# Inverse with the heads one below the other, rates as activations, the old state decayed ahead, and casts of y two K-tiles ahead

## The chip, the cores and the metric

The kernel runs on one core of a Trainium2 chip. The metric is the device time of one execution in microseconds, as a median over several runs. A profile of one execution tells what each engine did: TensorE (PE, with its weight loads PEld apart), VectorE (DVE), ScalarE (ACT), GpSimd (POOL) and SyncE (SP), which issues the DMAs.

## The reference, cut to what matters

One layer of a generator backbone, 256 latent tokens and 256 context tokens of width 2048, batch 1. A projection of the normalised input gives three groups of heads; the one that matters here is a bidirectional RWKV-7 recurrence with 16 heads of 64. Its scan runs over the tokens, for context first and then for the latents from the context's final state, forwards and backwards:

```
def step(s, inp):
    r_t, w_t, k_t, v_t, kk_t, a_t = inp
    sa = einsum('bhij,bhj->bhi', s, -kk_t)
    s = s * w_t[:, :, None, :] + sa[..., None] * (kk_t * a_t)[:, :, None, :] \
        + v_t[..., None] * k_t[:, :, None, :]
    return s, einsum('bhij,bhj->bhi', s, r_t)
...
a  = sigmoid(iclr_a0[d] + ad @ iclr_up[d])
kd = k * (1.0 + (a - 1.0) * k_a)
```

The outputs of both directions are added, group-normalised, gated, put beside a short convolution and a Fourier mix, and projected by `w_out`. A SwiGLU feed-forward part of width 5632 follows, and a last normalisation.

## The kernel before, in words

The program has four stages. Up to about 250 us it makes modulation vectors, the normalised input and the first projections. From about 250 to 1081 us runs `recurrence` (lines 851 to 900), which carries the change. From 1081 us on runs `phase_ffn`. Products with weights are made of three TensorE passes each: `wblock` (line 271) loads a block of weights by SyncE, casts it to a high part on ScalarE and subtracts for a low part on GpSimd or VectorE (`split`, line 264), and `mm3` runs high by high, high by low and low by high.

The recurrence works on pairs of heads, p = 0 to 7: head 0 of a pair lies on partitions 0 to 63, head 1 on 64 to 127 (`HV`, line 32). It first takes the eight pairs for the context (s = 0), then the eight for the latents (s = 1). A sequence of 256 tokens is cut into NC = 4 chunks of C = 64. For each of the 16 states, generators make the work:

- `rw_prep` (line 555) makes rates, decays and the small matrices of each chunk. At lines 614 to 619, for each direction and each of two operands, `f` is the rate on GpSimd (a multiply and an add with a column each), then its product on GpSimd, then `bk` on VectorE.
- `rw_inverse` (line 708), once for each direction, inverts a triangular 64x64 matrix for each chunk and head by five levels of doubling in f16, and then one correcting step in f32. `im` and `eb` hold the two heads of a chunk as the diagonal blocks of a 128x128 matrix whose other blocks were set to zero at the start (lines 859 to 862), so that one matmul of 128 rows serves both heads where they are the stationary operand. The products for the other operand (line 739) are 64*64, a head each. At the end of a level, ScalarE copies the results back in three casts (lines 743 to 745).
- `rw_scan` (line 765) goes over the four chunks in order, both directions at once: `rhs`, then `UV`, then the new state `w`. The new state is VectorE's sum of the product and the old state (line 812), times the decay of the chunk (line 813).
- `rw_out` and `group_norm` end a pair of the latents.

Each turn of the loop in `recurrence`, called a round here, takes one step of each live generator and then fills the round up to about 2.1 us of estimated TensorE time with steps of `fillers` (line 902): projections, the convolution, the Fourier mix, and `out_proj` (line 988). So TensorE's order is written out by hand by this loop. The orders of the other engines are a planner's, which follows the order of the program by priority and a simulated time; each of them runs its queue in order. `modvecs` (line 1050) puts products for the later modulation vectors (`macc`, line 1063) into VectorE's queue behind the last listed scan or inverse operation.

`out_proj` goes over the K-tiles of y in three parts, 8 to 15, 0 to 3 and 4 to 6, and then tile 7. Before each part it casts its K-tiles to `YH` (VectorE) and subtracts for `YL` (GpSimd), lines 1003 and 1004. `YH` and `YL` take over the buffers of the projections' input, `XH1` and `XL1`.

Of the kernel before, what the change touches and what calls it, by code (L numbers as in the profile page):

```python
# [17 lines left out]
P = 128  # L18
# [182 lines left out]
class Builder:  # L201
# [26 lines left out]
    def cst(self, name, i=0, n=None, rows=slice(0, P)):  # L228
        s, e = CC.at[name]
        return self.consts[rows, s + i:(e if n is None else s + i + n)]  # L230
# [324 lines left out]
    def rw_prep(self, st):  # L555
# [49 lines left out]
        for d in range(2):  # L605
            inc, exc, pi = exps[d]()
            aq = T(self.kv, [P, NC, 2 * C], F32, "aq", 4)
            st["AQ"].append(aq)
            V.tensor_tensor(aq[:, :, 0:C], exc, ch(kk), op=ALU.mult)
            if s:  # L610
                V.tensor_tensor(aq[:, :, C:], inc, ch(self.Y[:, p]), op=ALU.mult)
            bk = T(mp, [P, NC, 2, C], F32, "bk", 2)
            bks.append(bk)
            for i in range(2):
                f = T(mp, [P, L], F32, "f", 2)
                G.tensor_scalar(f, st["TA"][d], self.ab[:, 2 * i, p:p + 1], self.ab[:, 2 * i + 1, p:p + 1],
                                op0=ALU.mult, op1=ALU.add)
                G.tensor_tensor(f, f, u[i], op=ALU.mult)
                V.tensor_tensor(bk[:, :, i], ch(f), ch(pi), op=ALU.mult)
        yield 0.5  # L620
# [87 lines left out]
    def rw_inverse(self, st, d):  # L708

        nc, mp, cst = self.nc, self.mp, self.cst  # L710
        V, S, G, T = nc.vector, nc.scalar, nc.gpsimd, self.t
        while len(st["GA"]) <= d or self.inverted[d] < st["n"]:
            yield 0.0
        ga = st["GA"][d]
        msk = lambda l: self.bc4(self.m16[:, 6 * d + l])
        quads = [(c, h) for c in range(NC) for h in range(2)]
        im = self.im[d]
        x, eb = T(mp, [P, NC, C], F16, f"de{d}"), self.eb[d]
        for h in range(2):
            (G, V)[h].tensor_tensor(im[HV[h], :, h], ga[h][HV[h]], self.bc4(cst("i64", rows=HV[h])), op=ALU.add)  # L720
        for h in range(2):
            G.tensor_tensor(ga[h][HV[h]], ga[h][HV[h]], self.bc4(cst("i64", rows=HV[h])), op=ALU.add)
        yield 0.0
        pq = T(self.iv, [P, NC, C], F32, f"iv{d}")
        for c in range(NC):
            self.mm(pq[:, c], im[:, c].rearrange("p h t -> p (h t)"), self.i16, True, True)
        V.tensor_tensor(x, pq, msk(0), op=ALU.mult)
        for h in range(2):
            V.tensor_tensor(eb[HV[h], :, h], im[HV[h], :, h], self.bc4(self.m16[HV[h], 12 + d]), op=ALU.mult)  # L729
        yield 0.12  # L730
        sx = T(mp, [P, NC, C], F16, f"sx{d}")
        for l in range(1, 6):
            pd = T(self.iv, [P, 2, NC, C], F32, f"iv{d}")
            for c in range(NC):
                self.mm(pd[:, 0, c], im[:, c].rearrange("p h t -> p (h t)"), x[:, c], True, True)
            self.lastv = V.tensor_tensor(sx, pd[:, 0], msk(l), op=ALU.mult)
            yield 0.12
            for c, h in quads:
                self.mm(pd[HV[h], 1, c], sx[HV[h], c], eb[HV[h], c, h], True, True)
            for c in range(NC):  # L740
                self.mm(pd[:, 0, c], eb[:, c].rearrange("p h t -> p (h t)"), sx[:, c], True, True)
            if l < 5:
                S.copy(x, pd[:, 0])
                for h in range(2):
                    S.copy(eb[HV[h], :, h], pd[HV[h], 1])
            else:
                d32 = T(mp, [P, NC, C], F32, "d32")
                e32 = T(mp, [P, NC, C], F32, f"e32{d}", 2)
                S.copy(d32, pd[:, 0])
                S.copy(e32, pd[:, 1])  # L750
            yield 0.34
        pr = T(self.iv, [P, 2, NC, C], F32, f"iv{d}")
        for c, h in quads:
            self.mm(pr[HV[h], 0, c], ga[h][HV[h], c], d32[HV[h], c], True, True)
        r = T(mp, [P, NC, C], F32, "idm")
        V.tensor_tensor(r, self.bc4(cst("i64")), pr[:, 0], op=ALU.subtract)
        yield 0.6
        for c, h in quads:
            self.mm(pr[HV[h], 1, c], r[HV[h], c], e32[HV[h], c], True, True)
        V.tensor_tensor(e32, e32, pr[:, 1], op=ALU.add)  # L760
        st["E"][d] = e32
        self.inverted[d] += 1
        yield 0.6

    def rw_scan(self, st):

        nc, mp = self.nc, self.mp
        V, S, T = nc.vector, nc.scalar, self.t
        while self.done < st["n"] or None in st["E"]:
            yield 0.0  # L770
        yield 0.0
        p, s, UV, Z, AQ, E, BKT, PC = (st[k] for k in ("p", "s", "UV", "Z", "AQ", "E", "BKT", "PC"))
        W = self.wend[:, p] if s else None
        Ws = [W]
        for i in range(NC):
            cc = (i, NC - 1 - i)

            two = slice(i, 2 * NC - i, 2 * NC - 1 - 2 * i)
            zz = Z.rearrange("p d c t -> p (d c) t")[:, two]
            if W is None:  # L780
                rhs = zz
            else:
                pa = T(self.ps, [P, 2, C], F32, "st")
                for d in range(2):
                    for h in range(2):
                        self.mm(pa[HV[h], d], AQ[d][HV[h], cc[d], 0:C], W[HV[h], d], True, True)
                rhs = T(mp, [P, 2, C], F32, "rhs", 2)
                self.lastv = V.tensor_tensor(rhs, zz, pa, op=ALU.subtract)
                yield 0.29
            pu = T(self.ps, [P, 2, C], F32, "st")  # L790
            for d in range(2):
                for h in range(2):
                    self.mm(pu[HV[h], d], E[d][HV[h], cc[d]], rhs[HV[h], d], True, True)
            for h in range(2):
                u = UV[HV[h], h].rearrange("p d c t -> p (d c) t")[:, two]
                if h == 0:
                    self.lastv = V.tensor_copy(u, pu[HV[h]])
                else:
                    S.copy(u, pu[HV[h]])
            yield 0.29  # L800
            if s and i == NC - 1:
                break
            pw = T(self.ps, [P, 2, C], F32, "st")
            for d in range(2):
                for h in range(2):
                    self.mm(pw[HV[h], d], BKT[d][:, cc[d], C * h:C * h + C], UV[:, h, d, cc[d]], True, True)
            Wn = self.wend[:, p] if not s and i == NC - 1 else T(mp, [P, 2, C], F32, "w", 4)
            pc = PC[:, two].unsqueeze(2).to_broadcast([P, 2, C])
            if W is None:
                V.tensor_tensor(Wn, pw, pc, op=ALU.mult)  # L810
            else:
                V.tensor_tensor(Wn, pw, W, op=ALU.add)
                self.lastv = V.tensor_tensor(Wn, Wn, pc, op=ALU.mult)
            W = Wn
            Ws.append(W)
            yield 0.29
        if s:
            yield from self.rw_out(st, Ws)
        self.done += 1
        if s and p == 3:  # L820
            yield from self.group_norm(0, 4)
        if s and p == 6:
            yield from self.group_norm(4, 7)
        if s and p == 7:
            self.closing = True
            for _ in self.mv:
                pass
            yield from self.group_norm(7, 8)
# [22 lines left out]
    def recurrence(self):  # L851
# [3 lines left out]
        self.credit = 0.0  # L855
        self.normed = self.taken = self.valued = self.queried = self.done = 0
        self.inverted = [0, 0]

        self.im = [self.t(self.mp, [P, NC, 2, C], F16, f"im{d}") for d in range(2)]
        self.eb = [self.t(self.mp, [P, NC, 2, C], F16, f"eb{d}") for d in range(2)]  # L860
        for t in self.im + self.eb:
            self.nc.gpsimd.memset(t, 0.0)
        self.closing = self.gated = False
        for p in range(2):
            for _ in self.value(p):
# [122 lines left out]
    def out_proj(self):  # L988
# [11 lines left out]
        for k0, k1 in ((8, 16), (0, 4), (4, 7)):  # L1000
            while k0 < NP and self.normed < k1:
                yield None
            for k in range(k0, k1):
                self.split(YH[:, k], YL[:, k], self.Y[:, k], V, G)
            for n in range(KT):
                while k0 == 4 and (n >= HOLD and not self.closing or n >= KT - HOLD2 and self.normed < NP):
# [2 lines left out]
                for g in range(k0, k1, G4):  # L1009
                    m = min(G4, k1 - g)  # L1010
                    h, lo = self.wblock(self.a["wout"][n, :, g:g + m], m, G4, self.wst)
                    for j in range(m):
                        k = g + j
                        self.mm3(pj, h[:, j], lo[:, j], YH[:, k], YL[:, k], k == k0, k == k1 - 1)
                        yield MM3
                add(n, pj)
# [197 lines left out]
```

## Time and profile before

| | us |
|---|---|
| median of 3 runs | 1855.45 |
| lowest and highest run | 1853.03, 1862.34 |
| the profiled execution | 1853.2 |
| its span, first to last instruction | 1851.4 |
| TensorE busy | 1715.0 (93%) |
| TensorE weight loads busy | 1570.0 (85%) |
| VectorE busy | 1113.0 (60%) |
| ScalarE busy | 829.9 (45%) |
| GpSimd busy | 801.3 (43%) |
| mean granted clock of TensorE | 0.974 |

The profiled execution is one run of its own; its time is the span and what lies around it on the device. Matmuls are pipelined, so that the start of one group to the start of the next says what a group takes, and not its own length. An engine's idle time is put down to what ended it. Means over the span hide that the stages differ, so the stretch of the recurrence is read by itself.

### The profile page before, as it was taken

How to read it: one execution, taken by the hardware profiler on the slowest of the kernel's cores; microseconds unless marked ns; L12 is line 12 of the kernel's file. 1: busy time of each engine (PE TensorE's matmuls, PEld its weight loads, DVE VectorE, ACT ScalarE, POOL GpSimd, SP SyncE). 2: the span in 40 equal slices, each digit the busy share in tenths (PEclk: the TensorE clock that was granted, in tenths of full speed). 3: DMA queues.
4: the chain of work that ended last, by engine and by line, in shares of the span. 5: the costliest groups of instructions: out<-in, count | busy, mean ns of one | idle time of the engine just before them, and what ended most of it. 6: DMA issues, size and time to landing. Idle time of an engine off the chain costs nothing.

```text
span 1851.4 us, 44772 instructions
## 1 busy us (share of the span) xinstructions
PE 1715.0 (93%) x18552; PEld 1570.0 (85%) x18552; DVE 1113.0 (60%) x1883; ACT 829.9 (45%) x1657; POOL 801.3 (43%) x718
## 2 busy tenths in 40 slices
PE   7888999999899889898998888999999999999997
PEld 4767898888788777677786678999999999999996
DVE  4445257787888787768787488665555544333333
ACT  2113355566665554445554154444444444444442
POOL 1224455467667665656663353233222323333332
PEclk9999999999999999999999789999999999999998
DMA  9884224354545444344443137777777666565564
GB/s 335 305 273 152 75 78 129 121 161 149 160 153 159 141 135 133 107 156 137 128 134 100 46 114 233 238 240 241 231 231 231 200 194 191 186 188 189 188 188 137
DMA packets 139227, 318.74 MB, mean 172 GB/s; under 512 B 14224, under 2 KB 40464, under 8 KB 139024
## 3 DMA queue, kind: packets, MB, share of 16 engines
q1 hardware_dynamic: 137936, 314.84, 53.7%
q8 instruction: 145, 2.38, 0.5%
q10 hardware_dynamic: 1088, 1.05, 0.2%
q14 instruction: 58, 0.48, 0.1%
HBM read 313.74 MB, written 2.10 MB: 171 GB/s over the span
## 4 chain that ended last, share of the span: by engine, by line
PE 45%; DVE 8%; DMA 2%; ACT 2%; POOL 1%; issue 1%; DVEq 0%; ACTq 0%
PE gu L233 21%; PE dn L233 13%; PE pj L233 4%; DMA w<-wgu 2%; PE acc L233 2%; PE iv L233 2%; PE st L233 2%; POOL wlo L269 1%; PE pp L233 1%; DVE macc L1063 1%; DVE XL L1151 1%; ACT whi L266 1%; DVE HL L1122 0%; DVE eb L729 0%; DVE xn L1149 0%
## 5 line engine op out<-in xcount | busy, mean ns | idle before, releaser
L269 POOL TENSOR_TENSOR wlo<-w,whi 128x512 fp32r<-128x512 f32 (+2 forms) x309 | 518.6, 1681 | 712.8 <-ACT whi L266 679.7
L266 ACT CAST whi<-w 128x1024 fp32r<-128x1024 f32 (+2 forms) x472 | 401.2, 850 | 539.7 <-DMA w<-wgu 133.1
L233 PE MATMUL gu<-XH,whi 128*128 128x256 f32 (+1 forms) x1408 | 393.7, 280 | 4.2 <-ACT whi L266 3.7
L233 PE MATMUL gu<-XH,wlo 128*128 128x256 f32 (+1 forms) x1408 | 392.1, 280 | 3.6 <-POOL wlo L269 2.8
L269 DVE TENSOR_TENSOR wlo<-w,whi 128x1024 fp32r<-128x1024 f32 (+1 forms) x175 | 206.4, 1180 | 312.7 <-ACT whi L266 312.7
L233 PE MATMUL gu<-XL,whi 128*128 128x256 f32 x1344 | 372.5, 277 | 0.1
L233 PE MATMUL pj<-XH,whi 128*128 128x256 f32 x1016 | 286.5, 310 | 5.6 <-DVE XL L997 3.2
L233 PEld LDWEIGHTS gu<-XH,whi 128*128 128x128 f32 x1408 | 267.0, 190 | 5.9 <-ACT whi L266 5.2
L233 PEld LDWEIGHTS gu<-XH,wlo 128*128 128x128 f32 x1408 | 266.2, 190 | 4.6 <-POOL wlo L269 3.6
L233 PE MATMUL pj<-XL,whi 128*128 128x256 f32 x1016 | 258.5, 283 | 0.6 <-DVE XL L269 0.6
L233 PE MATMUL pj<-XH,wlo 128*128 128x256 f32 x1016 | 258.1, 282 | 0.0
L233 PEld LDWEIGHTS gu<-XL,whi 128*128 128x128 f32 x1344 | 253.8, 189 | 0.3 <-DVE XL L1151 0.3
L233 PEld LDWEIGHTS pj<-XH,whi 128*128 128x128 f32 x1016 | 182.5, 192 | 16.7 <-ACT whi L266 3.1
L233 PE MATMUL dn<-HL,whi 128*128 128x256 f32 x704 | 196.0, 278 | 0.0
L233 PE MATMUL dn<-HH,wlo 128*128 128x256 f32 x704 | 194.4, 276 | 0.0
L233 PE MATMUL dn<-HH,whi 128*128 128x256 f32 x704 | 194.3, 276 | 0.0
L233 PEld LDWEIGHTS pj<-XL,whi 128*128 128x128 f32 x1016 | 182.8, 192 | 2.4 <-issue 0.9
L233 PEld LDWEIGHTS pj<-XH,wlo 128*128 128x128 f32 x1016 | 181.8, 191 | 2.6 <-POOL whi L268 1.7
L1063 DVE SCALAR_TENSOR_TENSOR macc<-wm,sc,macc 128x512 f32<-128x512 f32 x180 | 169.9, 944 | 0.9
L233 PEld LDWEIGHTS dn<-HL,whi 128*128 128x128 f32 x704 | 132.1, 188 | 1.4
L233 PEld LDWEIGHTS dn<-HH,wlo 128*128 128x128 f32 x704 | 132.2, 188 | 0.0
L233 PEld LDWEIGHTS dn<-HH,whi 128*128 128x128 f32 x704 | 132.2, 188 | 0.0
(306 smaller groups left out, 2846.4 us busy)
## 6 DMA issues: line engine op xcount, KB each, us to landing
w<-wgu SPq DMA_DIRECT2D x176, 512.0 KB, 4.8
wm<-wmb SPq DMA_DIRECT2D x192, 256.0 KB, 3.1
w<-wdn SPq DMA_DIRECT2D x80, 512.0 KB, 4.4
w<-wib SPq DMA_DIRECT2D x148, 256.0 KB, 3.3
wm<-wma SPq DMA_DIRECT2D x64, 512.0 KB, 7.2
XH<-wmb SPq DMA_DIRECT2D x64, 256.0 KB, 5.0
w<-wout SPq DMA_DIRECT2D x48, 256.0 KB, 3.2
wa<-wia SPq DMA_DIRECT2D x16, 416.0 KB, 7.9
```

Of the source, the lines that this page charges most:

```text
L233: self.last = self.nc.tensor.matmul(out, lhsT=lhsT, rhs=rhs, start=start, stop=stop)
L266: he.copy(hi, src)
L269: le.tensor_tensor(lo, src, hi.bitcast(F32), op=ALU.subtract)
L1063: V.scalar_tensor_tensor(acc, w, self.sc[:, k, 1:2], acc, op0=ALU.mult, op1=ALU.add)
L1151: V.scalar_tensor_tensor(XL[:, k], xn, bias, XH[:, k].bitcast(F32), op0=ALU.add, op1=ALU.subtract)
```

## The change

The inverse holds the heads one below the other: `im` and `xe` (which joins `x` and `eb`) have the two heads on the two halves of the partitions and no zero blocks, and all f16 matmuls are 64*64, one for each chunk and head. The three casts of a level become one, the two masks on VectorE one, and the memsets go. The rates `f` are ScalarE activations with a scale and a bias column. In the scan, ScalarE multiplies the old state by its decay for each direction right after the state is made (`decayed`), and the new state is, for each direction, one VectorE operation: product times decay plus the decayed old state. In `out_proj` two K-tiles are cast ahead of the loop, and each further one two K-tiles before its use in the first block of columns.

```diff
--- before.py
+++ after.py
@@ -613,8 +613,8 @@
             bks.append(bk)
             for i in range(2):
                 f = T(mp, [P, L], F32, "f", 2)
-                G.tensor_scalar(f, st["TA"][d], self.ab[:, 2 * i, p:p + 1], self.ab[:, 2 * i + 1, p:p + 1],
-                                op0=ALU.mult, op1=ALU.add)
+                S.activation(f, st["TA"][d], AF.Identity, bias=self.ab[:, 2 * i + 1, p:p + 1],
+                             scale=self.ab[:, 2 * i, p:p + 1])
                 G.tensor_tensor(f, f, u[i], op=ALU.mult)
                 V.tensor_tensor(bk[:, :, i], ch(f), ch(pi), op=ALU.mult)
         yield 0.5
@@ -714,35 +714,34 @@
         ga = st["GA"][d]
         msk = lambda l: self.bc4(self.m16[:, 6 * d + l])
         quads = [(c, h) for c in range(NC) for h in range(2)]
-        im = self.im[d]
-        x, eb = T(mp, [P, NC, C], F16, f"de{d}"), self.eb[d]
+
+        im = T(mp, [P, NC, C], F16, f"im{d}")
         for h in range(2):
-            (G, V)[h].tensor_tensor(im[HV[h], :, h], ga[h][HV[h]], self.bc4(cst("i64", rows=HV[h])), op=ALU.add)
+            (G, V)[h].tensor_tensor(im[HV[h]], ga[h][HV[h]], self.bc4(cst("i64", rows=HV[h])), op=ALU.add)
         for h in range(2):
             G.tensor_tensor(ga[h][HV[h]], ga[h][HV[h]], self.bc4(cst("i64", rows=HV[h])), op=ALU.add)
         yield 0.0
         pq = T(self.iv, [P, NC, C], F32, f"iv{d}")
-        for c in range(NC):
-            self.mm(pq[:, c], im[:, c].rearrange("p h t -> p (h t)"), self.i16, True, True)
-        V.tensor_tensor(x, pq, msk(0), op=ALU.mult)
-        for h in range(2):
-            V.tensor_tensor(eb[HV[h], :, h], im[HV[h], :, h], self.bc4(self.m16[HV[h], 12 + d]), op=ALU.mult)
+        for c, h in quads:
+            self.mm(pq[HV[h], c], im[HV[h], c], self.i16[HV[h]], True, True)
+
+        xe = T(mp, [P, 2, NC, C], F16, f"de{d}")
+        V.tensor_tensor(xe[:, 0], pq, msk(0), op=ALU.mult)
+        V.tensor_tensor(xe[:, 1], im, self.bc4(self.m16[:, 12 + d]), op=ALU.mult)
         yield 0.12
         sx = T(mp, [P, NC, C], F16, f"sx{d}")
         for l in range(1, 6):
             pd = T(self.iv, [P, 2, NC, C], F32, f"iv{d}")
-            for c in range(NC):
-                self.mm(pd[:, 0, c], im[:, c].rearrange("p h t -> p (h t)"), x[:, c], True, True)
+            for c, h in quads:
+                self.mm(pd[HV[h], 0, c], im[HV[h], c], xe[HV[h], 0, c], True, True)
             self.lastv = V.tensor_tensor(sx, pd[:, 0], msk(l), op=ALU.mult)
             yield 0.12
             for c, h in quads:
-                self.mm(pd[HV[h], 1, c], sx[HV[h], c], eb[HV[h], c, h], True, True)
-            for c in range(NC):
-                self.mm(pd[:, 0, c], eb[:, c].rearrange("p h t -> p (h t)"), sx[:, c], True, True)
+                self.mm(pd[HV[h], 1, c], sx[HV[h], c], xe[HV[h], 1, c], True, True)
+            for c, h in quads:
+                self.mm(pd[HV[h], 0, c], xe[HV[h], 1, c], sx[HV[h], c], True, True)
             if l < 5:
-                S.copy(x, pd[:, 0])
-                for h in range(2):
-                    S.copy(eb[HV[h], :, h], pd[HV[h], 1])
+                S.copy(xe, pd)
             else:
                 d32 = T(mp, [P, NC, C], F32, "d32")
                 e32 = T(mp, [P, NC, C], F32, f"e32{d}", 2)
@@ -772,6 +771,16 @@
         p, s, UV, Z, AQ, E, BKT, PC = (st[k] for k in ("p", "s", "UV", "Z", "AQ", "E", "BKT", "PC"))
         W = self.wend[:, p] if s else None
         Ws = [W]
+        pcs = lambda i, d: PC[:, (2 * NC - 1 - i if d else i):(2 * NC - i if d else i + 1)]
+
+        def decayed(W, i):
+
+            w = T(mp, [P, 2, C], F32, "wp", 2)
+            for d in range(2):
+                S.mul(w[:, d], W[:, d], pcs(i, d))
+            return w
+
+        Wp = decayed(W, 0) if s else None
         for i in range(NC):
             cc = (i, NC - 1 - i)
 
@@ -805,14 +814,15 @@
                 for h in range(2):
                     self.mm(pw[HV[h], d], BKT[d][:, cc[d], C * h:C * h + C], UV[:, h, d, cc[d]], True, True)
             Wn = self.wend[:, p] if not s and i == NC - 1 else T(mp, [P, 2, C], F32, "w", 4)
-            pc = PC[:, two].unsqueeze(2).to_broadcast([P, 2, C])
             if W is None:
-                V.tensor_tensor(Wn, pw, pc, op=ALU.mult)
+                V.tensor_tensor(Wn, pw, PC[:, two].unsqueeze(2).to_broadcast([P, 2, C]), op=ALU.mult)
             else:
-                V.tensor_tensor(Wn, pw, W, op=ALU.add)
-                self.lastv = V.tensor_tensor(Wn, Wn, pc, op=ALU.mult)
+                for d in range(2):
+                    self.lastv = V.scalar_tensor_tensor(Wn[:, d], pw[:, d], pcs(i, d), Wp[:, d], op0=ALU.mult, op1=ALU.add)
             W = Wn
             Ws.append(W)
+            if i < NC - 1:
+                Wp = decayed(W, i + 1)
             yield 0.29
         if s:
             yield from self.rw_out(st, Ws)
@@ -855,11 +865,6 @@
         self.credit = 0.0
         self.normed = self.taken = self.valued = self.queried = self.done = 0
         self.inverted = [0, 0]
-
-        self.im = [self.t(self.mp, [P, NC, 2, C], F16, f"im{d}") for d in range(2)]
-        self.eb = [self.t(self.mp, [P, NC, 2, C], F16, f"eb{d}") for d in range(2)]
-        for t in self.im + self.eb:
-            self.nc.gpsimd.memset(t, 0.0)
         self.closing = self.gated = False
         for p in range(2):
             for _ in self.value(p):
@@ -1000,7 +1005,7 @@
         for k0, k1 in ((8, 16), (0, 4), (4, 7)):
             while k0 < NP and self.normed < k1:
                 yield None
-            for k in range(k0, k1):
+            for k in range(k0, k0 + 2):
                 self.split(YH[:, k], YL[:, k], self.Y[:, k], V, G)
             for n in range(KT):
                 while k0 == 4 and (n >= HOLD and not self.closing or n >= KT - HOLD2 and self.normed < NP):
@@ -1011,6 +1016,8 @@
                     h, lo = self.wblock(self.a["wout"][n, :, g:g + m], m, G4, self.wst)
                     for j in range(m):
                         k = g + j
+                        if n == 0 and k + 2 < k1:
+                            self.split(YH[:, k + 2], YL[:, k + 2], self.Y[:, k + 2], V, G)
                         self.mm3(pj, h[:, j], lo[:, j], YH[:, k], YL[:, k], k == k0, k == k1 - 1)
                         yield MM3
                 add(n, pj)
```

## Rows read from the trace of the kernel before

**Rows 1.** The page: busy us, share of the span, instructions.

```profile
PE 1715.0 (93%) x18552; PEld 1570.0 (85%) x18552; DVE 1113.0 (60%) x1883; ACT 829.9 (45%) x1657; POOL 801.3 (43%) x718
```

**Rows 2.** Stretches: length; PE, PEld, DVE, ACT, POOL busy; clock; DMA.

```profile
250.00:1000.00 750.00, 686.74 (x9345) 599.67 (x9344) 580.25 (x1150) 409.13 (x1043) 462.56 (x518) 0.97 0.45 138
```

**Rows 3.** TensorE's waits, 250 to 1000 us: total us, times, longest us.

```profile
PE iv L233 <- DVE idm L756: 20.4, 15, 3.5
PE st L233 <- DVE w L813: 11.2, 9, 5.3
...
PE st L233 <- ACT UV L799: 3.9, 6, 1.1
PE iv L233 <- ACT e L750: 3.9, 3, 1.8
```

**Rows 4.** TensorE in order of time, 303 to 309 us: start, length, group.

```profile
302.97 1.15 PE L233 MATMUL pp<-UV,ga 64*64 64x64 f32 x32
...
304.95 0.45 PE L233 MATMUL st<-w,aq 64*64 64x64 f32 x8
305.23 0.29 PE L233 MATMUL iv<-eb,sx 64*64 64x64 f16 x8
305.46 0.29 PE L233 MATMUL iv<-sx,eb 128*128 128x64 f16 x4
305.58 0.28 PE L233 MATMUL iv<-de,im 128*128 128x64 f16 x4
...
307.28 0.45 PE L233 MATMUL st<-rhs,e 64*64 64x64 f32 x8
307.66 0.29 PE L233 MATMUL iv<-de,im 128*128 128x64 f16 x4
307.88 0.31 PE L233 MATMUL iv<-eb,sx 64*64 64x64 f16 x8
```

**Rows 5.** TensorE in order of time, an f32 group of 256 columns.

```profile
792.71 1.89 PE L233 MATMUL pj<-XL 128*128 128x256 f32 x8
```

**Rows 6.** ScalarE's groups, whole span: shapes, count | busy us, mean ns | idle.

```profile
L745 ACT CAST eb<-iv 64x256 f16<-64x256 f32 x256 | 93.8, 366 | 3.1
L743 ACT CAST de<-iv 128x256 f16<-128x256 f32 x128 | 47.5, 371 | 70.4 <-PE iv L233 44.5 <-issue 15.1 <-ACT whi L266 7.6
L649 ACT COPY bkt<-pp 128x512 f32<-128x512 f32 x32 | 17.8, 588 | 31.5 <-PE pp L646 31.2
L468 ACT ACTIVATE xn<-xn,m 128x256 f32<-128x256 f32 x32 | 17.5, 592 | 123.6 <-DVE m L463 123.6
L799 ACT COPY UV<-st 64x128 f32<-64x128 f32 x64 | 16.7, 260 | 58.2 <-DVE UV L797 57.4
L684 ACT ACTIVATE ta<-pp,ha 128x256 f32<-128x256 f32 x32 | 14.9, 467 | 0.0
```

**Rows 7.** VectorE's and GpSimd's groups, whole span, same columns.

```profile
L729 DVE TENSOR_TENSOR eb<-im,m 64x256 f16<-64x256 f16 x64 | 34.5, 540 | 3.4 <-POOL im L720 1.6
L997 DVE SCALAR_TENSOR_TENSOR XL<-pj,mod,XL 128x256 f32<-128x256 f32 x56 | 26.7, 479 | 20.8 <-PE pj L233 20.3
L813 DVE TENSOR_TENSOR w<-w,pc 128x128 f32<-128x128 f32 x40 | 26.1, 652 | 0.6
L812 DVE TENSOR_TENSOR w<-st,w 128x128 f32<-128x128 f32 x32 | 9.2, 288 | 19.1 <-PE st L233 19.1
L1077 DVE TENSOR_TENSOR mod<-pj,vecs 128x4 f32<-128x4 f32 x12 | 1.9, 159 | 11.9 <-PE pj L233 11.9
...
L616 POOL TENSOR_SCALAR f<-ta,ab 128x256 f32<-128x256 f32 x64 | 50.6, 797 | 41.3 <-ACT ta L684 26.9 <-DVE bk L619 11.5 <-ACT tw L686 2.4
```

**Rows 8.** VectorE in order of time, 777 to 785 us.

```profile
777.76 2.43 DVE L268 CAST XH<-XH 128x256 fp32r<-128x256 f32 x5 [0.27 <-PE pj L233]
...
783.16 0.81 DVE L813 TENSOR_TENSOR w<-w,pc 128x128 f32<-128x128 f32 x1
```

**Rows 9.** A stretch after that wait, same columns as rows 2.

```profile
784.10:791.50 7.40, 7.39 (x54) 5.21 (x54) 3.43 (x7) 3.53 (x10) 3.07 (x6) 0.50 0.21 64
```

## The prediction

> **What bounds the kernel now.** I read the page's busy times first, then the stretches, then who waits for whom, then the orders of TensorE and VectorE themselves. The page shows TensorE busy 93% of the span [rows 1]. The change touches the recurrence alone, and nearly all of that lies between 250 and 1000 us. There TensorE is busy 686.74 of 750 us, VectorE 580.25, GpSimd 462.56, ScalarE 409.13 [rows 2]. So TensorE sets the pace, and 750 - 686.74 = 63 us of it is waiting. The waits are almost all for VectorE and ScalarE that come late: 20.4 us for `idm` of the inverse, 11.2 us for the new state `w` (one alone 5.3 us), 3.9 us each for `UV` and `e` [rows 3]. TensorE's own order is written out by hand, so a late operand stops all that stands behind it. Two things can therefore shorten the stage: fewer TensorE slots, and operands that come in time.
>
> **The change part by part.** All sums are against the profiled execution, 1853.2 us (span 1851.4, 1.8 us around it); the median of the runs is 2.25 us higher, 1855.45, and I add that at the end.
>
> *Heads one below the other, on TensorE.* Now each inverse has eleven groups of four 128-row matmuls with 64 columns (one for the transposition, two for each of five levels), 32 x 11 = 352. Each becomes eight 64*64 matmuls. Does twice the number cost twice the time? In the order of TensorE [rows 4] four 128-row ones take 305.46 to 305.58 = 0.12 us, and the eight 64*64 ones that exist already take 305.23 to 305.46 = 0.23 us. But this 0.23 holds a second thing. A group `st` of eight is followed by a 64*64 group after 0.28 us (304.95 to 305.23) and by a 128-row group after 0.38 us (307.28 to 307.66). A 128-row group is followed by a 64*64 one after 0.22 us (307.66 to 307.88), not 0.12. So a turn between the two shapes costs about 0.10 us in either direction, and eight 64*64 ones alone take 0.23 - 0.10 = 0.13 us: the two heads run beside each other. That they can is shown by f32: eight 128-row matmuls of 256 columns take 1.89 us, which is 0.236 each or 0.059 us for 64 columns [rows 5], while 32 64*64 ones of 64 columns take 1.15 us with their pipeline, 0.036 each [rows 4]. So the groups cost 352 x 0.01 = 3.5 us more, and what counts is the turns. Inside a level 128, 64, 128 become 64, 64, 64. Going through TensorE's order from 250 to 1085 us, I count 681 turns between neighbours without idle time between them; with every inverse group as 64*64 the same order has 483. A round such as that from 307.28 loses two of three turns; one such as that from 304.95 keeps one, since the turn moves behind the group. 198 x 0.10 = 20 us less. Together **-17 us**; bounds: -24 us (every turn at 0.12) and, if TensorE idles in those turns anyway, 0.
>
> A rule of the Trainium skill speaks against this: "TensorEngine Tiling (Array Packing)", section Instruction Overhead, gives each matmul a fixed cost of about 60 cycles and warns against tiling where the dimension is small already; at 64 columns eight small ones would then cost twice four. No row here separates issue from streaming; what it would make of the time is the last rival.
>
> *Heads one below the other, on ScalarE and VectorE.* At four levels of 32 inverses, three casts (371 + 2 x 366 = 1103 ns) become one of 128x512 [rows 6]. The nearest row is the copy of that size, 588 ns; upper end two 128x256 casts, 742. So 128 x 0.515 = 66 us of ScalarE go. The next level's first matmul needs the cast: 371 ns for `x` before, but `pd`'s buffer was free only after all three, so the new 588 ns is no later. On VectorE two masks of 540 ns become one of the same columns: 32 x 0.54 = 17 us go [rows 7]. The four memsets lie in the first stage beside GpSimd's idle time: nothing.
>
> *Rates as activations.* 64 GpSimd operations of 797 ns, 51 us, go; ScalarE gets 64 of 467 ns (nearest: `ta`, an activation with a bias column; ends 366, the cast of as many columns, and 592 [rows 6]), 30 us. This is the front of the chain rate, product, `bk`, behind which VectorE, in order, holds `e` and `idm`. I take **-5 us** of the 20.4 + 3.9 us of waits [rows 3]; ends 0 and -20.
>
> *Old state times its decay ahead.* 48 steps lose a sum of 288 and a product of 652 ns and get two `scalar_tensor_tensor` of 128x64 out of PSUM [rows 7]. No row has one; below is 159 ns (128x4), above 288 (128x128), and I take 240: on the line from 159 ns at 4 columns to the 479 ns of such an operation at 256, 64 columns give 235. The step's end comes 0.94 - 0.48 = 0.46 us earlier, and VectorE loses 22 us. Of the 11.2 us for `w` 5.9 remain beside the long one, in eight waits of about 0.7 us, and two like them lie in the tail after 1000 us: 10 x 0.4 = **-4 us**; ends 0 and -8. ScalarE gets 112 multiplications (8 heads' pairs x 3 steps x 2 and x 4 x 2, the last unused), 112 x 0.23 = 26 us, the duration between nothing and the 260 ns of the 64x128 copy. None is needed for three rounds, but each waits for VectorE's new `w`, and behind it on ScalarE stand the casts of weights and the evictions of `UV`, `iv` and `pp`. ScalarE's sum is -66 + 30 + 26 = -10 us, so its load does not grow, but its order gets new waits. I take **+2 us**; ends 0 and +44 (all 176 new operations at 0.25 us on the path).
>
> *Casts of y.* At 777.7 us the last reader of the buffer ends and VectorE casts five K-tiles in 2.43 us, two more follow, and only then it makes the state `w` (783.16) [rows 8], for which TensorE waits 5.3 us [rows 3]. The clock then stands at 0.50, the lower of its two levels, over 784.1 to 791.5 us, in which TensorE is busy 7.39 us [rows 9]; at the upper level the same work would take half, so up to 3.7 us more are lost. With two casts ahead and the others behind the first weight block, the product is ahead of most of them. **-6 us** of the at most -9; end 0 if the scheduler pulls the ready casts forward again. The two later bursts (four and three casts) come one by one already, as their tiles are finished.
>
> Sum: -17 - 5 - 4 + 2 - 6 = -30 us: 1853.2 - 30 = 1823 us profiled, and 1825 us as a median of runs. VectorE loses about 40 of 580 us, about as TensorE does, so VectorE stays as tight as it is: that is why I take only a quarter of the `idm` waits.
>
> **The rivals.** (1) *VectorE takes the pace.* It is busy 77% already, and its order is a planner's. If freed slots turn into waits of the same kind, half of the turns and the casts remain: -8 - 4 = -12, 1843 us. For: 63 us of waits in a stage that TensorE should bind. Against: each edit takes work off VectorE. (2) *Nothing comes through*: turns lie in front of waits, the casts bunch up again; 1850 to 1860 us. Against: the 681 turns counted are those without idle time. (3) *ScalarE in its order.* The multiplications wait for `w`, and evictions wait behind them. 112 + 64 operations at 0.25 us, all of it on the path, give +44 - 17 - 6 = +21: 1876 us. It decides against the change from about 27 us on, that is when six in ten of them delay something that TensorE takes next. For: the waits for `UV` and `e` show that ScalarE's evictions can be late. Against: ScalarE is busy 409 of 750 us. (4) *The small matmuls do not pair.* Eight at 0.03 us each, as the four 128-row ones are spaced, would also make 0.24 us, near the 0.23 seen; then each group costs 0.11 us more, 352 x 0.11 = +39 us, less the 13 us of the other parts: 1881 us. Against: the f32 rows, which cannot be had one by one.
>
> **How the numbers follow.** Forecast (1805 to 1840 us) 0.55; a gain smaller or larger that still counts, mostly rival 1, 0.18; rival 2 0.14; rivals 3 and 4 0.13 together. About 0.5%, 9 us, is what a measurement of this kernel can tell from no change. Below 1846 us lie the forecast and most of rival 1: faster 0.72. Same 0.15. Slower 0.13. The lower end is all terms at their ends but the waits for `idm` half: -24 - 10 - 8 - 9 = -51, 1804; I go to 1800. The upper end reaches over rival 1 into rival 2: 1851. The likeliest case's own range is 1805 to 1840.
>
> **What would show it.** In the trace after: a round of inverse groups between two `st` groups without the 0.38 us step, eight 64*64 groups following each other in 0.13 us, not 0.24 (else rival 4); one cast of about 0.6 us for each level; no wait of 5 us near 780 us and no half clock behind it; `w` made in two operations of at most 0.29 us; waits for `idm` below 20 us. If waits for ScalarE (`UV`, `e`, casts of weights) exceed 15 us, rival 3 is at work. If TensorE's waits in the recurrence stay above 60 us while its groups shorten, it is rival 1.

## The result and the profile after

The changed kernel takes 1835.52 us as a median (1833.69 to 1839.64, 4 runs), the kernel before beside it 1858.89 us. The ratio is 0.9879, with an interval of 0.9843 to 0.9914. A later run of the same program gave 1833.83 us and 0.9854 (0.9819 to 0.9889). So 22 to 27 us are gone, where 30 were forecast; 1835.5 us lies in the range of 1805 to 1840, ten above the 1825 that were named.

The page of the changed kernel, busy times as in [rows 1]:

```profile
PE 1702.9 (93%) x19960; PEld 1566.8 (86%) x19960; DVE 1068.0 (58%) x1851; ACT 827.7 (45%) x1577; POOL 744.5 (41%) x650
```

The recurrence's stretch after, columns of [rows 2]:

```profile
250.00:1000.00 750.00, 690.82 (x10997) 608.83 (x10996) 547.88 (x1135) 411.98 (x973) 410.11 (x457) 0.97 0.45 139
```

VectorE loses 32 us of this stretch, GpSimd 52, ScalarE gains 3; TensorE stays the one that paces, with 59 us of waiting instead of 63. But the 750 us hold more of the work than before, so the stage is better taken whole. From the first inverse matmul to the first of the feed-forward part it was 258.43 to 1081.53 us, and is 258.89 to 1064.08: 823.1 us became 805.2. These two stretches, before and then after, columns of [rows 2]:

```profile
258.43:1081.53 823.10, 747.49 (x9996) 644.98 (x9995) 617.56 (x1240) 434.97 (x1105) 476.42 (x530) 0.96 0.43 130
```

```profile
258.89:1064.08 805.19, 736.63 (x11404) 642.50 (x11403) 578.35 (x1207) 430.91 (x1020) 422.79 (x469) 0.96 0.44 133
```

TensorE is busy 10.9 us less and waits 7.0 us less (75.6 to 68.6). The feed-forward part is 2 us shorter, without any edit in it. So 18 of the 19.5 us between the two spans come from the recurrence.

TensorE in order of time after, start, length, group:

```profile
439.49 0.45 PE L233 MATMUL st<-rhs,e 64*64 64x64 f32 x8
439.77 0.29 PE L233 MATMUL iv<-de,sx 64*64 64x64 f16 x8
439.89 0.29 PE L233 MATMUL iv<-sx,de 64*64 64x64 f16 x8
440.02 0.29 PE L233 MATMUL iv<-de,im 64*64 64x64 f16 x8
440.24 0.39 PE L233 MATMUL pj<-XH,whi 128*128 128x256 f32 x1
```

Eight 64*64 matmuls take 0.12 and 0.13 us when another 64*64 group follows, and 0.22 us when `pj` with 128 rows follows. That is the turn of 0.10 us, now behind the groups. Between neighbours without idle time I count 500 turns from 250 us to the end of the recurrence, where 681 were and 483 were forecast. The count hangs on what is called a turn: by every change of rows or columns it is 888 before and 732 after, by a change of columns alone 619 and 468, so 151 to 181 turns are gone.

Waits of TensorE after, 250 to 1000 us, columns of [rows 3]:

```profile
PE iv L233 <- DVE idm L755: 25.3, 14, 4.2
PE iv L233 <- DVE de L729: 6.0, 6, 2.2
...
PE iv L233 <- ACT de L744: 4.3, 9, 1.6
...
PE st L233 <- DVE w L821: 3.0, 3, 2.1
PE st L233 <- ACT UV L808: 2.1, 4, 0.8
PE iv L233 <- ACT e L749: 1.0, 2, 0.7
```

The wait for the state fell from 11.2 to 3.0 us, those for ScalarE's `UV` and `e` by 4.7 us together; the one for a level's cast is 4.3 us (2.2 before, for `eb`), and the one for `idm` rose from 20.4 to 25.3.

The new operations on ScalarE and VectorE, columns of [rows 6] and [rows 7]:

```profile
L744 ACT CAST de<-iv 128x512 f16<-128x512 f32 x128 | 74.2, 579 | 29.9 <-PE iv L233 19.7 <-issue 3.7 <-ACT whi L266 2.1
L616 ACT ACTIVATE f<-ta,ab 128x256 f32<-128x256 f32 x64 | 35.9, 598 | 5.1 <-DVE bk L619 5.0
L780 ACT ACTIVATE wp<-w,pc 128x64 f32<-128x64 f32 x96 | 30.3, 344 | 40.2 <-DVE w L821 31.9 <-DVE w L818 8.2
```

```profile
L730 DVE TENSOR_TENSOR de<-im,m 128x256 f16<-128x256 f16 x32 | 20.3, 634 | 2.9 <-POOL im L720 1.1
L821 DVE SCALAR_TENSOR_TENSOR w<-st,pc,wp 128x64 f32<-128x64 f32 x80 | 18.9, 277 | 19.9 <-PE st L233 19.9
```

### The profile page after: what moved, and what is told of

Same layout as the page of the kernel before. It is cut to its first block, busy times and chain, and to the rows that moved or that the text cites. A ratio compares the mean times of both kernels' runs of the same rounds, so it can differ in the third digit from the quotient of the medians.

```text
span 1831.9 us, 47450 instructions
## 1 busy us (share of the span) xinstructions
PE 1702.9 (93%) x19960; PEld 1566.8 (86%) x19960; DVE 1068.0 (58%) x1851; ACT 827.7 (45%) x1577; POOL 744.5 (41%) x650
## 4 chain that ended last, share of the span: by engine, by line
PE 72%; DVE 14%; ACT 5%; issue 4%; POOL 1%; DMA 0%; DVEq 0%; ACTq 0%; POOLq 0%
PE gu L233 25%; PE pj L233 17%; PE dn L233 13%; PE iv L233 4%; PE pp L233 4%; PE st L233 3%; PE acc L233 3%; DVE macc L1070 2%; PE pacc L233 1%; DVE m L463 1%; DVE im L720 1%; DVE XL L1158 1%; DVE bk L619 1%; ACT xn L468 1%; DVE HL L1129 1%
## 5 line engine op out<-in xcount | busy, mean ns | idle before, releaser
L269 POOL TENSOR_TENSOR wlo<-w,whi 128x512 fp32r<-128x512 f32 (+2 forms) x309 | 515.4, 1671 | 750.2 <-ACT whi L266 722.9
L233 PE MATMUL pj<-XH,whi 128*128 128x256 f32 x1016 | 290.9, 315 | 3.3 <-DVE XL L1002 1.6
L1070 DVE SCALAR_TENSOR_TENSOR macc<-wm,sc,macc 128x512 f32<-128x512 f32 x180 | 163.9, 910 | 1.9 <-DMA wm<-wmb 1.1
```

What stands on the lines that cost most here:

```text
L233: self.last = self.nc.tensor.matmul(out, lhsT=lhsT, rhs=rhs, start=start, stop=stop)
L269: le.tensor_tensor(lo, src, hi.bitcast(F32), op=ALU.subtract)
L1070: V.scalar_tensor_tensor(acc, w, self.sc[:, k, 1:2], acc, op0=ALU.mult, op1=ALU.add)
```

## The experiments

Each time is a median of 5 to 12 executions, beside the kernel before on the same chip. Runs under one heading shared a chip, but for the last one; over chips, ratios are compared, since the median of before lay between 1855.24 and 1860.68 us.

### The four parts one at a time

The inverse alone:

```diff
-            for c in range(NC):
-                self.mm(pd[:, 0, c], im[:, c].rearrange("p h t -> p (h t)"), x[:, c], True, True)
+            for c, h in quads:
+                self.mm(pd[HV[h], 0, c], im[HV[h], c], xe[HV[h], 0, c], True, True)
...
-                S.copy(x, pd[:, 0])
-                for h in range(2):
-                    S.copy(eb[HV[h], :, h], pd[HV[h], 1])
+                S.copy(xe, pd)
```

> The kernel before with the new inverse alone (64*64 f16 matmuls, one cast a level, one mask, no zero blocks). Theory (TensorE's turns): about 180 of 681 turns between the shapes go at 0.10 us, 352 groups cost 0.01 us more: 12 to 18 us faster than before, so most of the 22 us of the whole change. Rival (VectorE's relief): the gain comes from VectorE's shorter queue, of which this part has 17 us of 45: less than 9 us faster, and TensorE's waits grow by what the turns give.

Measured: 1849.75 us, 0.9937 (0.9914 to 0.9961), against 1859.69.

The decay alone (buffer single):

```diff
+            w = T(mp, [P, 2, C], F32, "wp", 1)
+            for d in range(2):
+                S.mul(w[:, d], W[:, d], pcs(i, d))
...
-                V.tensor_tensor(Wn, pw, W, op=ALU.add)
-                self.lastv = V.tensor_tensor(Wn, Wn, pc, op=ALU.mult)
+                for d in range(2):
+                    self.lastv = V.scalar_tensor_tensor(Wn[:, d], pw[:, d], pcs(i, d), Wp[:, d], op0=ALU.mult, op1=ALU.add)
```

> The kernel before with the old state decayed ahead alone (its buffer single instead of double, for space). Theory: the waits for the state w fall from 11 us to about 3, of which some come back as other waits: 3 to 8 us faster. Rival (VectorE's relief): this part takes 21 us off VectorE, the most of all parts: 9 us or more faster.

Measured: 1861.73 us, 1.0021 (0.9986 to 1.0056): no gain, against theory and rival alike.

The rates alone:

```diff
-                G.tensor_scalar(f, st["TA"][d], self.ab[:, 2 * i, p:p + 1], self.ab[:, 2 * i + 1, p:p + 1],
-                                op0=ALU.mult, op1=ALU.add)
+                S.activation(f, st["TA"][d], AF.Identity, bias=self.ab[:, 2 * i + 1, p:p + 1],
+                             scale=self.ab[:, 2 * i, p:p + 1])
```

> The kernel before with the rates as ScalarE activations alone. Theory: GpSimd was not what TensorE waited for, and the product behind the rate still stands on GpSimd: within 4 us of before, either sign, waits for idm not below 18 us. Rival (VectorE's relief): VectorE's operations with two SBUF operands shorten without 51 us of GpSimd beside them: 5 us or more faster.

Measured: 1867.05 us, 1.0046 (1.0019 to 1.0073): slower, by about 8 us, more than the theory allowed; and the waits for `idm` fell below its 18 us.

The casts alone:

```diff
-            for k in range(k0, k1):
+            for k in range(k0, k0 + 2):
...
+                        if n == 0 and k + 2 < k1:
+                            self.split(YH[:, k + 2], YL[:, k + 2], self.Y[:, k + 2], V, G)
```

> The kernel before with the casts of y two K-tiles ahead alone. Theory: the planner still takes the ready casts as soon as their buffer is free, seven of eight within 8 us as in the changed kernel: within 3 us of before, and a wait of TensorE of several us near 780 us stays. Rival: the two-ahead order itself took 5.3 to 2.1 us of that wait and shortened the half clock: 4 to 9 us faster.

Measured: 1864.31 us, 1.0009 (0.9976 to 1.0041), with the wait of 5.3 us still there: no gain, as the theory says, though the median is 4.6 us above that of before.

What follows: only the inverse gains alone, 12 us by the ratio (7 to 16) and 10 by the medians, the least of what the turns promised. That is above the rival's bound of 9, but the interval reaches below it. The other three together give 0.0076 of loss, so the four alone add up to 1.0013, but together they gave 0.9879 and 0.9854. Neither theory had this: the parts depend on each other. The recurrence itself, from its first inverse matmul to the first feed-forward one, says the same; it is taken from one profiled execution each, and two of the same program differ by 3.7 us. The feed-forward part, which no edit touches, took 787 and 786 us in the traces of the decay and the casts alone and 770 in that of the kernel before, so whole times scatter for reasons outside the change. The clock is the mean granted clock over all executions that were timed, with that of the kernel before beside it.

| | recurrence, us | TensorE busy | waiting | clock | clock of before |
|---|---|---|---|---|---|
| before | 823.1 | 747.5 | 75.6 | | |
| inverse alone | 819.5 | 746.3 | 73.2 | 0.9662 | 0.9719 |
| decay alone | 825.4 | 757.4 | 68.0 | 0.9691 | 0.9719 |
| rates alone | 828.3 | 750.2 | 78.1 | 0.9701 | 0.9719 |
| casts alone | 819.4 | 743.3 | 76.2 | 0.9733 | 0.9719 |
| changed kernel | 805.2 | 736.6 | 68.6 | | |
| the same again | 808.9 | 743.8 | 65.0 | 0.9722 | 0.9712 |

The granted clock is a rival that no run puts to the test. The inverse alone ran at a lower clock than the kernel before, and the decay alone took 7.6 us of waiting away and had 9.9 us more of busy TensorE. An estimate from this table: if TensorE loses what the mean clock loses, the four alone lose 0.0089 of the time to it in sum, while the whole change gains 0.0010. That is 18 us of the 25 to 30 by which the sum of the parts misses the whole. No run parts the clock from the waits, so which of them comes first stays open.

Waits of TensorE with the rates alone, 250 to 1000 us:

```profile
PE iv L233 <- DVE idm L756: 17.2, 13, 2.2
...
PE st L233 <- ACT UV L799: 6.8, 10, 1.8
PE iv L233 <- ACT eb L745: 6.3, 11, 1.7
```

The last two were 3.9 us [rows 3] and 2.2 us before. ScalarE is busy 436 us of the stretch there instead of 409. That gave the next theory: the rates and the multiplications need room on ScalarE, and the merged cast makes it. For the multiplications the trace does not bear it out: with the decay alone ScalarE is busy 436 us too, and the waits for `UV` and `eb` there are 2.5 and 2.3 us.

### The parts taken out of the changed kernel

First the changed kernel again:

> The changed kernel as it is, on the same chip as the next three. Every theory: as measured, about 0.988 of before.

Measured: 1833.83 us, 0.9854 (0.9819 to 0.9889), against 1860.68.

Without the rates (the diff above reversed):

> The changed kernel with the rates back on GpSimd. Theory (ScalarE's room): alone the rates cost 8 us because ScalarE, 30 us fuller, came late with UV and the casts; in the changed kernel the merged cast pays for that, so taking them back changes little: 0.986 to 0.991 of before. Rival (the parts add): 8 us faster than the changed kernel, 0.984 or less of before. Second rival (the parts need each other through VectorE): slower than the changed kernel, 0.992 or more.

Measured: 1844.29 us, 0.9920 (0.9896 to 0.9943). The second rival's bound is met: in the changed kernel the rates are worth about 10 us by the medians, 8 to 12 by the ratios. Its waits:

```profile
PE iv L233 <- DVE idm L755: 25.9, 18, 3.1
PE iv L233 <- DVE sx L737: 6.4, 10, 1.7
```

The wait for `sx` was 3.9 us with the rates on ScalarE; the waits for ScalarE are 5.6 us in sum here and 8.1 there. So the room on ScalarE says why the rates cost nothing in the changed kernel, and not what they gain. The clock was 0.9690, against 0.9722 for the changed kernel on the same chip, an estimated 6 us of the 10.

Without the decay ahead:

> The changed kernel with the old two VectorE operations for the new state. Theory (ScalarE's room): alone it gave nothing because 35 us of multiplications went to ScalarE; with room there the shorter path shows: 4 to 8 us slower than the changed kernel, 0.990 to 0.993 of before. Rival (the parts add): alone it gave nothing, so nothing is lost: 0.986 to 0.989.

Measured: 1837.68 us, 0.9879 (0.9847 to 0.9912), 4 us by the medians, with intervals that overlap: at the theory's lower edge in us and within the rival's range in the ratio, so open. The long wait for the state is back:

```profile
PE st L233 <- DVE w L812: 8.5, 8, 5.5
```

With three casts a level:

```diff
-                S.copy(xe, pd)
+                S.copy(xe[:, 0], pd[:, 0])
+                for h in range(2):
+                    S.copy(xe[HV[h], 1], pd[HV[h], 1])
```

> The changed kernel with each level's cast in three pieces again, 64*64 matmuls and all else kept: ScalarE gets 66 us back. Theory (ScalarE's room): the evictions come late again and at least 8 us of the gain go: 0.992 or more of before, waits for ScalarE's casts and UV over 12 us. Rival (TensorE's turns are all): the turns are kept and ScalarE is off the path: 0.987 to 0.990.

Measured: 1845.44 us, 0.9920 (0.9890 to 0.9950), as the theory says. Its waits for ScalarE:

```profile
PE iv L233 <- ACT de L746: 13.7, 19, 2.2
...
PE iv L233 <- ACT e L751: 2.0, 4, 0.8
PE pj L233 <- ACT u L574: 2.0, 1, 2.0
PE st L233 <- ACT UV L810: 1.7, 2, 1.2
```

The turns are the same there and the matmuls too, and the clock, 0.9714, is nearly that of the changed kernel. So about 11 us of the inverse's worth in the changed kernel is the merged cast, by way of ScalarE. Two ways lead there, and no run parts them: 59 us less of load on ScalarE in the stretch (471 to 412), or the end of a level's copies, for which the next level's first matmul waits, 0.5 us sooner (three casts, 1103 ns together, against one of 579).

### The theory of room, the casts held, and idm

Three casts and the rates on GpSimd at once:

> The changed kernel with each level's cast in three pieces and with the rates on GpSimd. Taken back singly, each cost 0.0066 of the time. Theory (ScalarE's room: the rates pay only while ScalarE has room for them): without room there is nothing to lose with the rates, so both together cost about as much as one: 0.990 to 0.994 of before, waits for ScalarE 10 to 14 us as in the kernel before. Rival (two separate gains): both are lost, 0.997 or more.

Measured: 1845.78 us, 0.9948 (0.9926 to 0.9970), against 1855.24. Taken one by one the two cost 0.0066 each; both cost 0.0094 in the ratio against 0.9854. It lies between one loss (0.9920) and two (0.9986), just beyond the theory's 0.994 and short of the rival's 0.997; the interval holds both. The waits for a level's cast are 8.5 us, less than with three casts and the rates on ScalarE (13.7). So the rates seem to pay less where ScalarE is full; whether they pay nothing there stays open. No run has the turns alone either. This one comes nearest, with the turns, the decay, the single mask and the casts of y: 0.9948 is 10 us, 6 to 14 by the interval, where the turns counted below make 12 to 15; but its clock was 0.9696 where before had 0.9747.

The casts of y held behind the scan:

```diff
+                            with self.tc.issue_after(self.lastv.ins):
+                                self.split(YH[:, k + 2], YL[:, k + 2], self.Y[:, k + 2], V, G)
```

> The changed kernel with each cast of y that is made in the loop held behind the last scan operation recorded before it, so that the planner cannot take five at once. Theory (the casts bunched up because they were ready): the waits near 770 to 790 us for w, sx and the cast of a level (2.1, 0.7, 0.7 and 1.6 us) and the half clock behind them go: 3 to 8 us faster than the changed kernel, 0.981 to 0.984 of before. Rival (they only move: VectorE is as full either way): within 2 us of the changed kernel.

Measured: 1837.70 us, 0.9915 (0.9885 to 0.9945). Now two casts stand at 771 us and the others at 784 to 789 us, and the ratio is no lower than that of the changed kernel (0.9854 and 0.9879), if anything a little higher. The theory is out. That they only move, as the rival says, fits the recurrence in the traces (804.6 us against 805.2 and 808.9); the ratio is above the rival's bound of 2 us.

The products for the modulation vectors behind `idm`:

```diff
-        V.tensor_tensor(r, self.bc4(cst("i64")), pr[:, 0], op=ALU.subtract)
+        self.lastv = V.tensor_tensor(r, self.bc4(cst("i64")), pr[:, 0], op=ALU.subtract)
...
-        V.tensor_tensor(e32, e32, pr[:, 1], op=ALU.add)
+        self.lastv = V.tensor_tensor(e32, e32, pr[:, 1], op=ALU.add)
```

> The changed kernel with the products for the modulation vectors queued also behind idm and the last sum of an inverse, the two operations for which TensorE waits longest; macc stands among the three operations ahead of idm 13 times instead of 31. Theory (TensorE waits for idm because VectorE's queue holds macc before it): the waits for idm fall from 25 us to 15 or less, 5 to 12 us faster than the changed kernel. Rival (idm waits behind bk, which waits for GpSimd's product): waits for idm stay above 20 us and the time within 3 us.

Measured: 1825.03 us (1823.13 to 1828.06), 0.9837 (0.9807 to 0.9867), 12.7 us below the run with the casts held on the same chip. It is below the changed kernel too, by 3 to 8 us in the ratios, with intervals that overlap. Its recurrence took 794.4 us in the trace, against 804.6 with the casts held and 805.2 and 808.9 in the changed kernel. The clock was 0.9738, against 0.9705 with the casts held. Its waits:

```profile
PE iv L233 <- DVE idm L755: 9.1, 8, 2.7
PE pp L233 <- DVE mq L639: 7.4, 7, 3.0
```

More of the same:

```diff
-                V.tensor_tensor(gt, pg[:, :, 0:C], ...
+                self.lastv = V.tensor_tensor(gt, pg[:, :, 0:C], ...
...
-                    V.tensor_tensor(mq[:, h], pg[:, :, C:], ...
+                    self.lastv = V.tensor_tensor(mq[:, h], pg[:, :, C:], ...
...
-        V.tensor_tensor(xe[:, 1], im, ...
+        self.lastv = V.tensor_tensor(xe[:, 1], im, ...
```

> The changed kernel with macc queued behind idm and the last sum of an inverse, and further behind the masks ga and mq of the preparation and the second mask of an inverse. In the three operations ahead macc now stands 7 times instead of 19 before mq and 26 instead of 58 before ga, but 45 instead of 29 times before the first masks of an inverse. Theory (each wait goes that macc is taken away from): the 11 us of waits for mq halve, 3 to 6 us faster than with idm alone, about 0.981 of before. Rival (macc has to stand before something): the waits for the masks of the inverse grow by as much, within 3 us of the run with idm alone, 0.982 to 0.986.

Measured: 1829.67 us, 0.9850 (0.9820 to 0.9880), against 1856.11. Nothing is gained over `idm` alone. The wait for `mq` shown above fell from 7.4 to 3.8 us, and others came, though not those that the rival expected:

```profile
PE st L233 <- ACT UV L808: 8.9, 10, 2.5
PE st L233 <- DVE rhs L797: 7.2, 5, 2.6
PE st L233 <- DVE w L818: 6.4, 3, 2.5
```

## Why the prediction came out, point by point

**The turns (-17 us).** The mechanism held in the trace: 0.12 to 0.13 us for eight, 0.22 before a turn, 151 to 181 turns gone where 198 were forecast. At 0.10 us each, less 352 x 0.01, that is 12 to 15 us; TensorE's busy time in the recurrence fell by 10.9 us, in the second profiled execution by 3.7. Two small slips in the prediction change nothing: its own terms, 20 less 3.5, make 16 and not 17, and 0.236 us for an f32 matmul is the length of a group, with its pipeline, by eight; from start to start it is 0.22. The rule of a fixed cost for each matmul, in the Trainium skill's "TensorEngine Tiling (Array Packing)", section Instruction Overhead, taken by itself would have had the eight cost twice the four; the trace does not agree for pairs that lie on different halves of the array, so rival 4 is out. The inverse alone, merged cast included, measured 12 us; what the turns alone bring in time no run shows.

**ScalarE's sum and the merged cast.** The cast measured 579 ns (588 taken). The rates measured 598 ns, above the upper end of 592, and the multiplications 344 ns, above their upper end of 260. So ScalarE was not relieved by 10 us, its busy time stayed (409 to 412 us in the stretch). The prediction put the cast's relief off the path. That step failed: with three casts 11 us come back, and the waits for ScalarE are 22 us instead of 8, over the mark of 15 that rival 3 had; the changed kernel stays under it. Whether that is ScalarE's load or the later end of a level's copies stays open.

**Rates (-5 us for `idm`).** Half right alone, wrong in the whole. With the rates alone the wait for `idm` fell by 3.2 us, and more came back as waits for ScalarE. In the changed kernel it is 25.3 us with them and 25.9 without, and yet they are worth 10 us there and cost 8 us alone. `bk`, which was to come sooner, takes longer: 701 ns in the mean, 635 before. Moving work to another engine had no fixed price here. Part of it is how full that engine was, part the clock, and the rest is open.

**The decay (-4 us).** The waits for `w` fell by 8.2 us, of which 3.2 us are in the one long wait near 780 us; the operation takes 277 ns instead of 240. Taken out, it costs 4 us by the medians, alone it gave nothing. The shorter path to the state is shown, and the forecast size is not contradicted; that it gains time is not shown.

**The casts (-6 us).** Wrong; the end at nothing, which the prediction named, is what happened. VectorE in order of time after:

```profile
769.77 2.40 DVE L268 CAST XH<-XH 128x256 fp32r<-128x256 f32 x5 [0.28 <-PE pj L233]
772.10 0.46 DVE L821 SCALAR_TENSOR_TENSOR w<-st,pc,wp 128x64 f32<-128x64 f32 x2
772.48 0.96 DVE L268 CAST XH<-XH 128x256 fp32r<-128x256 f32 x1
```

The planner takes five ready casts at once as in [rows 8]. What shortened the longest wait for the state from 5.3 to 2.1 us was the decay ahead: the state's two operations stand side by side there, with no cast between. With the casts alone it stayed at 5.3 us; with the decay alone, 250 to 1000 us, it was 1.9 us:

```profile
PE st L233 <- DVE w L822: 3.3, 3, 1.9
```

The lower clock behind that wait, which was to go, did not. It stood at 0.50 for 10.2 us from 781.3 us on before, and after for 3.4 us from 775.1 us on and in this stretch, columns of [rows 2]:

```profile
785.30:792.10 6.80, 6.29 (x74) 5.93 (x74) 4.21 (x8) 3.30 (x9) 1.05 (x3) 0.50 1.07 359
```

**The waits for `idm` (rival 1).** They stayed because VectorE's order stayed. VectorE, then GpSimd and then TensorE, after, before the longest of them:

```profile
417.84 0.74 DVE L1070 SCALAR_TENSOR_TENSOR macc<-wm,sc,macc 128x512 f32<-128x512 f32 x1
...
418.89 2.81 DVE L619 TENSOR_TENSOR bk<-f,sm 128x256 f32<-128x256 f32 x2
421.62 0.41 DVE L759 TENSOR_TENSOR e<-e,iv 128x256 f32<-128x256 f32 x1
421.95 0.41 DVE L755 TENSOR_TENSOR idm<-consts,iv 128x256 f32<-128x256 f32 x1
```

```profile
418.75 2.67 POOL L269 TENSOR_TENSOR wlo<-w,whi 128x512 fp32r<-128x512 f32 x2 [0.61 <-ACT whi L266]
```

```profile
422.42 1.12 PE L233 MATMUL iv<-e,idm 64*64 64x64 f32 x16 [4.21 <-DVE idm L755]
```

`idm` stands behind `macc` and two `bk`, and these two take 2.81 us while GpSimd subtracts from 418.75 to 421.42 us; the mean of one `bk` is 0.70, the median 0.42. The Trainium skill's "SBUF — State Buffer", section "SBUF: two separate sides", says that a VectorE operation with two SBUF inputs and a GpSimd operation that reads SBUF lock each other out for a whole instruction; this stretch agrees, though no run here took the GpSimd operation away. With `macc` moved the waits fell to 9.1 us, and the time by 12.7 us on the same chip: the stage was open to such a gain, and the change did not touch it. This is rival 1 in part: TensorE's waits in the stretch stayed at 59 us, one below its mark of 60.

In sum, over the recurrence of the two traces: TensorE busy -10.9 us and waiting -7.0, against -17 and -13 forecast. The 12 us that are missing are the casts, the waits for `idm`, which grew, and part of the turns; on the other side the waits for the state and for `UV` and `e` fell further than forecast. So the range was right, and the way there only in part. Two terms that were put at nothing or wrongly, the merged cast and the rates, turned out to be worth 11 and 10 us in the whole, and one of -6 was nothing. That the total still came near is in part luck.

## What to carry to other kernels

Matmuls of half the rows and columns, a pair on different halves, cost as little here as full ones with zero blocks (0.12 to 0.13 us for eight, 0.12 for four), and what they save is the turn between the two shapes: count the turns in the order. What moved work is worth depends on the rest of the change, so parts are to be tried by taking each out of the whole, not only alone: here one part cost 8 us alone and gave 10 us in company. Set the granted clock of the runs beside their times before a difference is put down to waits. Where a planner orders an engine's queue, a cast that is written later is still taken early if it is ready; and a long accumulation that no one waits for belongs behind the operation that the pacing engine takes next.

## What was not expected of the hardware

An activation of 128x256 with a scale and a bias column, out of SBUF, took 598 ns: the row of the same form (592) was the one to go by, and not the one out of PSUM with a bias column alone (467) [rows 6]. One of 128x64 with a scale column took 344 ns, more than a copy of twice the columns on half the partitions (260) [rows 6]. The second mask of an inverse, of 128x256 f16, took 634 ns where two of 64x256 took 540 each [rows 7]. The mean granted clock differed by kernel on one chip, 0.9662 for the inverse alone and 0.9719 for the kernel before. Three of four parts measured alone were not faster, and the whole was, by more than the one that was.
